# Two blocks of keys made behind the queries, closer steps in the attention, and two output blocks in turn

## The chip, the cores and the metric

One core of one Trainium2 chip runs the whole program. The metric is the device time in microseconds (us) of one execution, and lower is better. The engines are TensorE (PE, with PEld for its weight loads), VectorE (DVE), ScalarE (ACT), GpSimd (POOL) and SyncE (SP), which issues the loads of the weights.

## The reference

The reference is a two-layer decoder trunk on 256 positions and a width of 2048, in float32. Layer one is a retention layer with an MLP; layer two is a multi-head latent attention (MLA) with an MLP. The part that the change touches is the MLA of layer two, with 16 heads:

```python
kv = (c_kv @ w_kv_up).reshape(b, s, MLA_HEADS, MLA_NOPE_DIM + MLA_V_DIM)
k_nope = rms_norm(kv[..., :MLA_NOPE_DIM], k_nope_norm)
v = kv[..., MLA_NOPE_DIM:]
...
c_q = rms_norm(h @ w_dq, q_norm)
q = (c_q @ w_uq).reshape(b, s, H, MLA_NOPE_DIM + MLA_ROPE_DIM)
q_nope = rms_norm(q[..., :MLA_NOPE_DIM], q_nope_norm)
q_pe = apply_rope(rms_norm(q[..., MLA_NOPE_DIM:], q_pe_norm), cos[:, :, None], sin[:, :, None])
...
p = jax.nn.softmax(sc, axis=-1).astype(v.dtype)
return jnp.einsum('bhqk,bkhd->bqhd', p, v)
```

The scores sc are the products of q_nope with k_nope plus those of q_pe with the one rotary key k_pe, masked causally. The result of all heads goes through w_o and is added to the residual stream.

## The kernel before, in words

All products in this stage run as three matmuls: a float32 operand is split into a high half in fp32r and the rest, the low half (split, line 188: ACT makes the high half at L191, DVE the low half at L192). Weights come in pieces. stream (L214) loads one piece with a DMA on SP's queue and splits it in two halves of which each has a tile wh and a tile wl; there are five buffers of each and four of the raw piece. piece (L241) multiplies a half in 12 matmuls (L252 to L254), so a piece has 24. A block is a product with one set of columns over all pieces (gemm, L412).

Around the pieces, steps of other work are put in by hand. later(n, fn) (L99) queues a step that is due n pieces from now; tick (L107) is called at the end of each piece and runs what is due; need(items, n) (L112) runs queued steps early when a piece wants an operand that isn't there. This makes the order in which the program is written; the build then sets the order within each engine, so that matmuls of a step can stand between those of a piece.

The attention goes in blocks of two heads, b = 0 to 7. In the order of the program:

- The keys and values: eight blocks of one piece each, with 512 columns (chunks of mla_w_kv_up, tiles ku). keyed (L960) copies keys (kn) and values (v) out of PSUM on ACT, sums squares on DVE (L972, L973), takes the root on POOL (kn_r, L181), scales the keys (L978), and two pieces later transposes them (kntp) and splits them into kt (L194, L195).
- The queries: eight blocks of three pieces each, with 384 columns (mla_w_uq, tiles uq). query (L997) runs at a block's end: ACT copies the queries out (qs, L1002) and their squares (qu, L1004), DVE sums them (sq, L1005 and L1006), POOL takes the root (qn_r), and DVE scales and rotates (L1013, L864 to L867, L1022, L1023, tiles qs, qu, qpp).
- Three pieces later its turn (L1026) transposes both parts on PE (qntp, qptp), and ACT and DVE make qt (a raw tile and its two halves) and qpe.
- Three pieces after that, score (L1039) makes 20 matmuls into s (L1049 to L1054), DVE adds the mask into p (L1059) and takes the negated maximum mx (L1064), ACT takes the exponential with its sums (L1069), DVE the reciprocal, and ACT scales (L1075).
- Three pieces later its turn (L1077) transposes p (ptp, L1082) and ACT copies it (pt, L1084); two pieces after that, values (L1090) makes ao (L1093, L1094) and splits it into ot (L191, L192), which is appended to o_act.
- The output block: gemm_blocks (L424) multiplies o_act with mla_w_o, in four blocks of 512 columns with four pieces each (tiles wo). The first two blocks share a start: three pieces of block 0, three of block 1, then the last piece of each. Piece g needs 2g + 2 entries of o_act. x_tiles (L139) brings the residual stream back with DMAs that POOL issues (L146).

Transposes, ptp and ao share two PSUM banks under the tag "tp", taken in turn; products of weights share four ("acc"); s takes a pair of banks of its own, of which there is one.

Of the kernel before, what the change touches and what calls it, by code (L numbers as in the profile page):

```python
# [68 lines left out]
def yoco(ctx: ExitStack, tc: tile.TileContext, a):  # L69
# [7 lines left out]
    def small(w, name):  # L77
        return pool.tile([P, w], F32, tag="small", bufs=36, name=name)
# [20 lines left out]
    def later(n, fn):  # L99
        queue.append((clock[0] + n, next(count), fn))  # L100
# [311 lines left out]
    def gemm(w, chunk0, act, nk, nb, name, done, before=None):  # L412

        acc = accs(nb, name)
        n = nk // 4
        for g in range(n - 1):
            piece(w, chunk0 + g, acc, act, g, nk, nb, name, before)
        last_piece(w, chunk0, acc, act, nk, nb, name, done, before)
# [5 lines left out]
    def gemm_blocks(w, chunk_of, act, nk, name, done):  # L424

        n = nk // 4
        first = [accs(512, f"{name}{b}") for b in range(2)]
        for b in range(2):
            for g in range(n - 1):
                piece(w, chunk_of(b) + g, first[b], act, g, nk, 512, f"{name}{b}")  # L430
        for b in range(2):
            last_piece(w, chunk_of(b), first[b], act, nk, 512, f"{name}{b}", lambda acc, b=b: done(b, acc))
        for b in range(2, NB):
            gemm(w, chunk_of(b), act, nk, 512, f"{name}{b}", lambda acc, b=b: done(b, acc))
# [436 lines left out]
    rc, ckv = [], []  # L871
# [88 lines left out]
    def keyed(acc, b):  # L960
        if b % 2 == 0:
            vs.append(act_tile(f"v{b}", F32))
        vt = vs[-1][:, b % 2].rearrange("p t (h c) -> p t h c", h=2)
        v_s.append(vt)
        kr = []
        s2 = small(2 * NT, f"skn{b}").rearrange("p (t i h) -> p t i h", t=NT, i=1)
        for t in range(NT):
            src = acc[t].rearrange("p (h c) -> p h c", h=2)
            k = f2k([2, 2, NOPE], f"kn{b}{t}")
            nc.scalar.activation(k[:, 0], src[:, :, 0:NOPE], AF.Copy, scale=rc[t])  # L970
            nc.scalar.activation(vt[:, t], src[:, :, NOPE:], AF.Copy, scale=rc[t])
            nc.vector.tensor_tensor(k[:, 1], k[:, 0], k[:, 0], op=ALU.mult)  # L972
            nc.vector.reduce_sum(s2[:, t, 0], k[:, 1], axis=AX.X)  # L973
            kr.append(k)
        rn = rstds(s2, [NOPE], f"kn{b}")
        for t in range(NT):
            k = kr[t]
            nc.vector.tensor_tensor(  # L978
                k[:, 1], k[:, 0], rn[:, t, 0].unsqueeze(2).to_broadcast([P, 2, NOPE]), op=ALU.mult
            )  # L980

        def turn():
            tp = transposed(lambda t, j: kr[t][:, 1, j], f"kntp{b}")
            kt = act_tile(f"kt{b}")
            split(kt[:, 0], kt[:, 1], tp, gain(G_KN))
            k_t.append(kt)

        later(2, turn)

    for b in range(8):  # L990
        gemm(a["mla_w_kv_up"], b, ckv, 4, 512, f"ku{b}", lambda acc, b=b: keyed(acc, b))


    nc.vector.tensor_scalar(gqn, gain(G_QN), scale, None, op0=ALU.mult)
    o_act = []

    def query(acc, b):  # L997
        qr, qu = [], []
        sq = small(4 * NT, f"sq{b}").rearrange("p (t i h) -> p t i h", t=NT, i=2)
        for t in range(NT):  # L1000
            q = f2k([2, 192], f"qs{b}{t}")
            nc.scalar.activation(q.rearrange("p h c -> p (h c)"), acc[t], AF.Copy, scale=rq[t])  # L1002
            u = f2k([2, 192], f"qu{b}{t}")
            nc.scalar.activation(u.rearrange("p h c -> p (h c)"), acc[t], AF.Square, scale=rq[t])  # L1004
            nc.vector.reduce_sum(sq[:, t, 0], u[:, :, 0:NOPE], axis=AX.X)  # L1005
            nc.vector.reduce_sum(sq[:, t, 1], u[:, :, NOPE:], axis=AX.X)  # L1006
            qu.append((q, u))
        r = rstds(sq, [NOPE, ROPE], f"qn{b}")
        for t in range(NT):
            q, u = qu[t]  # L1010
            for i, cols in enumerate((slice(0, NOPE), slice(NOPE, NOPE + ROPE))):
                n = cols.stop - cols.start
                nc.vector.tensor_tensor(  # L1013
                    q[:, :, cols], q[:, :, cols], r[:, t, i].unsqueeze(2).to_broadcast([P, 2, n]), op=ALU.mult
                )
            flat = u.rearrange("p h c -> p (h c)")
            pe = flat[:, 0 : 2 * ROPE]
            tmp = flat[:, 2 * ROPE : 4 * ROPE].rearrange("p (h c) -> p h c", h=2)
            pe_rope(pe.rearrange("p (h c) -> p h c", h=2), tmp, q[:, :, NOPE:], t, 1, 2)
            parts = f2k([2, 2, ROPE], f"qpp{b}{t}", F32R)  # L1020
            pe = pe.rearrange("p (h c) -> p h c", h=2)
            nc.vector.tensor_copy(parts[:, :, 0], pe)  # L1022
            nc.vector.tensor_tensor(parts[:, :, 1], pe, parts[:, :, 0].bitcast(F32), op=ALU.subtract)  # L1023
            qr.append((q, parts.bitcast(F32)))

        def turn():  # L1026
            tp = transposed(lambda t, j: qr[t][0][:, j, 0:NOPE], f"qntp{b}")
            raw = f2k([2, S], f"qt{b}")
            nc.scalar.activation(raw, tp, AF.Copy, scale=gqn)
            qt = [f2k([2, S], f"qt{b}{i}", F32R) for i in range(2)]  # L1030
            split(qt[0], qt[1], raw)
            tp = transposed(lambda t, j: qr[t][1][:, j].rearrange("p i c -> p (i c)"), f"qptp{b}")
            qpe = f2k([2, S], f"qpe{b}", F32R)
            nc.scalar.copy(qpe, tp)
            later(3, lambda: score(b, qt, qpe))

        later(3, turn)

    def score(b, qt, qpe):  # L1039

        sc = two_banks(f"s{b}")
        for hh in range(2):
            for t in range(NT):
                dst = sc[:, hh, t * P : t * P + (t + 1) * P]
                qs = slice(t * P, (t + 1) * P)
                n = (t + 1) * P
                qh, ql = (i[:, hh, qs] for i in qt)
                kh, kl = (k_t[b][:, i, hh, :n] for i in range(2))
                nc.tensor.matmul(dst, qh, kh, start=True, stop=False)  # L1049
                nc.tensor.matmul(dst, qh, kl, start=False, stop=False)  # L1050
                nc.tensor.matmul(dst, ql, kh, start=False, stop=False)

                for i in range(2):
                    nc.tensor.matmul(dst, qpe[:, hh, qs], kpe_t[:, i, :n], start=False, stop=i == 1)  # L1054
        p = [f2k([2, (t + 1) * P], f"p{b}{t}") for t in range(NT)]
        for t in range(NT):
            cols = slice(t * P, t * P + (t + 1) * P)
            cut = mask[:, cols].unsqueeze(1).to_broadcast([P, 2, (t + 1) * P])
            nc.vector.tensor_tensor(p[t], sc[:, :, cols], cut, op=ALU.add)  # L1059
        neg = small(4, f"mx{b}")  # L1060
        den = small(4, f"den{b}")
        inv = small(4, f"inv{b}")
        for t in range(NT):
            nc.vector.tensor_reduce(neg[:, 2 * t : 2 * t + 2], p[t], axis=AX.X, op=ALU.max, negate=True)  # L1064
        for t in range(NT):
            for hh in range(2):
                i = 2 * t + hh
                view = p[t][:, hh]
                nc.scalar.activation(view, view, AF.Exp, bias=neg[:, i : i + 1], accum_out=den[:, i : i + 1])  # L1069
        nc.vector.reciprocal(inv, den)  # L1070
        for t in range(NT):
            for hh in range(2):
                i = 2 * t + hh
                view = p[t][:, hh]
                nc.scalar.activation(view, view, AF.Copy, scale=inv[:, i : i + 1])  # L1075

        def turn():  # L1077
            pt = []
            for hh in range(2):
                tp = bank("tp", [3 * P], f"ptp{b}{hh}")  # L1080
                for i, src in enumerate((p[0][:, hh], p[1][:, hh, 0:P], p[1][:, hh, P:])):
                    nc.tensor.transpose(tp[:, i * P : (i + 1) * P], src, ident)  # L1082
                o = f2k([3 * P], f"pt{b}{hh}")
                nc.scalar.copy(o, tp)  # L1084
                pt.append(o)
            later(2, lambda: values(b, pt))

        later(3, turn)

    def values(b, pt):  # L1090
        o = bank("tp", [2, S], f"ao{b}")
# [7 lines left out]
    for b in range(8):  # L1099
        gemm(a["mla_w_uq"], b * 3, cq, 12, Q_NB, f"uq{b}", lambda acc, b=b: query(acc, b))  # L1100

    ss = [small(NB, f"ss3_{t}") for t in range(NT)]
    act, r = [], []
    x_tiles("wo")
# [104 lines left out]
```

## Time and profile before

| what | us |
|---|---|
| median of 3 runs | 2476.02 (2473.25 to 2478.36) |
| the profiled execution | 2474.57 |
| its span in the trace | 2472.8 |
| keys and values, PE from - to | 1505 - 1552 |
| queries and attention, PE from - to | 1552 - 1684 |
| output block, PE from - to | 1684 - 1789 |

Times in the trace count from the start of the span. PE counts as busy from the start of a matmul to its modelled end, and matmuls overlap: the distance from one start to the next tells how fast they go. A line of the view of waits names the instruction that waited, what it waited for, the total, the number of times and the longest. In the windows each engine has its busy time and the number of instructions, then come PE's granted clock and the DMA share. The chain of waits names at each step the link that came last; its pieces are cut where the next one takes over, so its lengths add up.

### The profile page before, as it was taken

To read this page: it belongs to the slowest core of one execution; us is meant where nothing else is said; L and a number is where in the kernel's file an instruction comes from. 1 tells how busy PE (TensorE), PEld (TensorE's weight loads), DVE (VectorE), ACT (ScalarE), POOL (GpSimd) and SP (SyncE) were. 2 spreads that over 40 slices of the span, in tenths; PEclk is the share of its full clock that TensorE was granted. 3 is DMA by queue.
4 is the path that set the end of the run, shared out by engine and by line. 5 is a ranking of instruction groups with operands and counts; after the bars stand their busy time and mean duration, and the time that the engine had idled before them with its cause. 6 is when DMAs were issued, how large, how long until landed. Compare 5 with 4: busy or idle time off the path is not lost.

```text
span 2472.8 us, 31782 instructions
## 1 busy us (share of the span) xinstructions
PE 2456.4 (99%) x11635; PEld 2057.7 (83%) x11635; DVE 2187.8 (88%) x2842; ACT 1616.3 (65%) x2275; POOL 249.3 (10%) x310
## 2 busy tenths in 40 slices
PE   9999999999999999999999999999999999999999
PEld 7888888888888888888888888998888888888887
DVE  7799999889899999999999988776689999999996
ACT  6566656556676667667666767676566666676663
POOL 7300011000010010110110101110000201101100
PEclk9999999999999999999999999999999999999999
DMA  9545567555565685684775555445645856857854
GB/s 327 212 173 206 185 206 242 194 194 206 198 235 182 209 262 215 208 258 172 247 262 200 191 208 189 153 154 179 199 175 199 262 212 207 269 202 226 265 193 153
DMA packets 93980, 521.05 MB, mean 211 GB/s; under 512 B 11136, under 2 KB 12288, under 8 KB 40576
## 3 DMA queue, kind: packets, MB, share of 16 engines
q1 hardware_dynamic: 72288, 472.56, 53.4%
q0 software_dynamic: 21248, 46.15, 8.5%
q8 instruction: 91, 1.49, 0.2%
q14 instruction: 65, 0.53, 0.1%
q10 hardware_dynamic: 288, 0.31, 0.0%
HBM read 479.14 MB, written 39.85 MB: 210 GB/s over the span
## 4 chain that ended last, share of the span: by engine, by line
PE 90%; DVE 5%; ACT 3%; issue 1%; POOL 1%; DMA 1%; SPq 0%; ACTq 0%; DVEq 0%; POOLq 0%
PE u_c L364 7%; PE u_c L363 7%; PE u_c L362 7%; PE d_c L364 6%; PE d_c L362 6%; PE d_c L363 6%; PE rk_acc L280 2%; PE rq_acc L280 2%; PE rp_c L362 2%; PE rp_c L363 2%; PE rp_c L364 2%; PE u_p L364 2%; PE u_p L363 2%; PE u_p L362 2%; PE d_p L362 2%; PE d_p L364 2%
## 5 line engine op out<-in xcount | busy, mean ns | idle before, releaser
L191 ACT CAST u_wh<-u_raw 128x1024 fp32r<-128x1024 f32 x362 | 348.1, 991 | 207.8 <-DVE u_raw L327 100.7
L191 ACT CAST d_wh<-d_raw 128x1024 fp32r<-128x1024 f32 x358 | 344.3, 993 | 202.6 <-DVE d_raw L327 94.0
L192 DVE TENSOR_TENSOR u_wl<-u_raw,u_wh 128x1024 fp32r<-128x1024 f32 x362 | 401.6, 1142 | 47.4 <-ACT u_wh L191 41.8
L192 DVE TENSOR_TENSOR d_wl<-d_raw,d_wh 128x1024 fp32r<-128x1024 f32 x358 | 397.4, 1144 | 40.3 <-ACT d_wh L191 35.6
L362 PE MATMUL u_c<-u_wh,n 128*128 128x512 f32 x706 | 276.4, 392 | 0.0
L363 PE MATMUL u_c<-u_wl,n 128*128 128x512 f32 x706 | 275.5, 390 | 0.0
L364 PE MATMUL u_c<-u_wh,n 128*128 128x512 f32 x706 | 275.0, 390 | 0.0
L362 PE MATMUL d_c<-d_wh,hid 128*128 128x512 f32 x654 | 256.0, 391 | 0.0
L363 PE MATMUL d_c<-d_wl,hid 128*128 128x512 f32 x654 | 255.3, 390 | 0.0
L364 PE MATMUL d_c<-d_wh,hid 128*128 128x512 f32 x654 | 254.8, 390 | 0.0
L191 ACT CAST rp_wh<-rp_raw 128x1024 fp32r<-128x1024 f32 (+1 forms) x166 | 160.7, 982 | 140.0 <-DVE rp_raw L327 64.6
L192 DVE TENSOR_TENSOR rp_wl<-rp_raw,rp_wh 128x1024 fp32r<-128x1024 f32 (+1 forms) x166 | 184.6, 1135 | 26.0 <-ACT rp_wh L191 23.7
L364 PEld LDWEIGHTS u_c<-u_wh,n 128*128 128x128 f32 x706 | 132.6, 188 | 27.3
L362 PEld LDWEIGHTS u_c<-u_wh,n 128*128 128x128 f32 x706 | 132.5, 188 | 27.1
L363 PEld LDWEIGHTS u_c<-u_wl,n 128*128 128x128 f32 x706 | 132.6, 188 | 26.7
L364 PEld LDWEIGHTS d_c<-d_wh,hid 128*128 128x128 f32 x654 | 122.8, 188 | 25.4
L362 PEld LDWEIGHTS d_c<-d_wh,hid 128*128 128x128 f32 x654 | 122.8, 188 | 25.1
L363 PEld LDWEIGHTS d_c<-d_wl,hid 128*128 128x128 f32 x654 | 122.8, 188 | 24.7
L156 POOL DMA_DIRECT2D xh<-d_c x48 | 41.6, 867 | 856.4 <-ACT d_c L379 854.4
L191 ACT CAST ro_wh<-ro_raw 128x1024 fp32r<-128x1024 f32 x88 | 85.7, 997 | 59.5 <-DVE ro_raw L327 25.6
L362 PE MATMUL rp_c<-rp_wh,a 128*128 128x512 f32 x286 | 111.8, 391 | 0.0
L363 PE MATMUL rp_c<-rp_wl,a 128*128 128x512 f32 x286 | 111.4, 390 | 0.2 <-DVE rp_wl L192 0.2
(515 smaller groups left out, 6100.7 us busy)
## 6 DMA issues: line engine op xcount, KB each, us to landing
u_raw<-in_mlp_w SPq DMA_DIRECT2D x128, 1024.0 KB, 5.3
d_raw<-in_mlp_w SPq DMA_DIRECT2D x120, 1024.0 KB, 4.9
rp_raw<-in_ret_w_gv SPq DMA_DIRECT2D x56, 1024.0 KB, 4.8
ro_raw<-in_ret_w_out SPq DMA_DIRECT2D x32, 1024.0 KB, 4.9
uq_raw<-in_mla_w_uq SPq DMA_DIRECT2D x24, 768.0 KB, 4.1
rq_raw<-in_ret_w_qk SPq DMA_DIRECT2D x16, 1024.0 KB, 5.2
rk_raw<-in_ret_w_qk SPq DMA_DIRECT2D x16, 1024.0 KB, 4.9
wo_raw<-in_mla_w_o SPq DMA_DIRECT2D x16, 1024.0 KB, 4.8
```

The lines of the kernel that those rows point to most:

```text
L156: nc.gpsimd.dma_start(x_home[t][2 * p + j], part, accum_op=ALU.add)
L191: nc.scalar.copy(h, src)
L192: nc.vector.tensor_tensor(l, src, h.bitcast(F32), op=ALU.subtract)
L280: nc.tensor.matmul(acc[f], wh[:, cols], a.rearrange("p i s -> p (i s)"), start=k == 0, stop=k == nk - 1)
L362: nc.tensor.matmul(dst, ah, bh, start=n == 0, stop=False)
L363: nc.tensor.matmul(dst, ah, bl, start=False, stop=False)
L364: nc.tensor.matmul(dst, al, bh, start=False, stop=n == total[key] - 1)
```

## The change

Three edits. The keys and values of blocks 6 and 7 are made behind the last block of queries instead of ahead of the first. The distances of the attention's four steps, which were 3, 3, 3 and 2 pieces, are 3, 2, 3 and 2 for blocks 0 to 5, 3, 4, 2 and 1 for block 6 and 2, 2, 2 and 2 for block 7. The first two output blocks take their first three pieces in turn. Lines behind L990 have numbers some five higher in the changed kernel.

```diff
         first = [accs(512, f"{name}{b}") for b in range(2)]
-        for b in range(2):
-            for g in range(n - 1):
+        for g in range(n - 1):
+            for b in range(2):
                 piece(w, chunk_of(b) + g, first[b], act, g, nk, 512, f"{name}{b}")
...
-    for b in range(8):
-        gemm(a["mla_w_kv_up"], b, ckv, 4, 512, f"ku{b}", lambda acc, b=b: keyed(acc, b))
+    def keys(heads):
+        for b in heads:
+            gemm(a["mla_w_kv_up"], b, ckv, 4, 512, f"ku{b}", lambda acc, b=b: keyed(acc, b))
+
+    keys(range(6))
...
+    waits = [(3, 2, 3, 2)] * 6 + [(3, 4, 2, 1), (2, 2, 2, 2)]
...
-            later(3, lambda: score(b, qt, qpe))
+            later(waits[b][1], lambda: score(b, qt, qpe))
 
-        later(3, turn)
+        later(waits[b][0], turn)
...
-            later(2, lambda: values(b, pt))
+            later(waits[b][3], lambda: values(b, pt))
 
-        later(3, turn)
+        later(waits[b][2], turn)
...
     for b in range(8):
         gemm(a["mla_w_uq"], b * 3, cq, 12, Q_NB, f"uq{b}", lambda acc, b=b: query(acc, b))
 
+
+    keys((6, 7))
     ss = [small(NB, f"ss3_{t}") for t in range(NT)]
```

## The prediction

> **What bounds the kernel now.** Read first the page's busy line and its chain that ended last, then what TensorE (PE) waited for, then the windows of the attention stage.
>
> ```profile
> PE 2456.4 (99%) x11635; PEld 2057.7 (83%) x11635; DVE 2187.8 (88%) x2842; ACT 1616.3 (65%) x2275; POOL 249.3 (10%) x310
> PE 90%; DVE 5%; ACT 3%; issue 1%; POOL 1%; DMA 1%; SPq 0%; ACTq 0%; DVEq 0%; POOLq 0%
> ```
>
> ```profile
> PE qptp L211 <- DVE ot L192: 1.9, 1, 1.9
> ...
> PE qptp L211 <- ACT qt L1029: 1.1, 1, 1.1
> ...
> PE wo_acc L252 <- ACT ot L191: 0.3, 1, 0.3
> ```
>
> ```profile
> 1505.00:1552.40 47.40, 47.40 (x226) 39.27 (x225) 39.45 (x78) 33.46 (x61) 9.54 (x11) 1.00 0.43 150
> ...
> 1610.00:1630.00 20.00, 18.09 (x116) 17.41 (x116) 15.65 (x43) 15.32 (x34) 2.31 (x1) 1.00 0.40 146
> ...
> 1645.18:1662.88 17.70, 17.70 (x115) 17.48 (x114) 13.59 (x37) 12.66 (x29) 2.31 (x1) 1.00 0.42 147
> ...
> 1681.00:1735.00 54.00, 52.44 (x287) 44.86 (x286) 31.66 (x58) 33.60 (x71) 4.86 (x7) 1.00 0.51 176
> ```
>
> PE is the bound, at a granted clock of 1.00. The change keeps every matmul, so all it can win is PE's idle time from the keys to the second output block: 20.00 - 18.09 = 1.91 us, and 54.00 - 52.44 = 1.56 us. That is **3.5 us**; with the matmuls that run on at a slower pitch around these waits I take 4.0. A block of queries (two heads, b = 0 to 7) costs PE **17.70 us**, and in the window of one it never waits. The other engines are idle for 4 us of it, so their sum is no limit. Their order may be. These are the pieces of the chain of waits in which PE is not the link:
>
> ```profile
> 1662.56 0.58 ACT qs L1002
> 1663.14 0.47 ACT qu L1004
> 1663.61 0.47 ACT qs L1002
> 1664.08 0.48 ACT qu L1004
> ...
> 1664.59 0.42 DVE sq L1005
> ...
> 1665.55 2.25 POOL qn_r L181
> 1667.83 0.96 DVE qs L1013 x3
> ...
> 1671.46 0.87 DVE uq_wl L192
> 1672.33 0.60 DVE qt L192
> 1672.93 0.93 DVE p L1059 x2
> 1673.86 0.34 DVE mx L1064
> 1674.22 1.87 ACT p L1069 x8
> ...
> 1676.93 1.49 ACT p L1075 x4
> ```
>
> PE's own timeline of the same block:
>
> ```profile
> 1662.88 0.60 PE L211 MATMUL qntp<-cst,qs 128*128 128x128 f32 x4
> ...
> 1663.67 0.31 PE L1049 MATMUL s<-kt,qt 128*128 128x128 f32 x1
> ...
> 1663.93 0.27 PE L1051 MATMUL s<-kt,qt 128*128 128x128 f32 x1
> ...
> 1666.05 0.34 PE L252 MATMUL uq_acc<-uq_wh,cq 128*128 128x384 f32 x1
> ...
> 1675.09 0.59 PE L1093 MATMUL ao<-pt,v 128*128 128x256 f32 x2
> ...
> 1676.31 0.42 PE L252 MATMUL uq_acc<-uq_wh,cq 128*128 128x384 f32 x1
> ```
>
> The scores s leave PE at 1666.05, yet VectorE (DVE) adds their mask (p) at 1672.93, behind this block's roots, qs, a weight low (uq_wl) and the low half of qt. It takes its work as it stands, and p is late by 7 us. That costs nothing now: the scores that p reads were made long before, from the qt of an earlier round. So no link of this chain comes back to PE.
>
> **The change part by part.**
>
> *Steps 3, 2, 3, 2.* Scores now come two pieces behind their transposes instead of three, in the same round in which qt is made. In the changed program PE runs: transposes of block b, 57 rows of the next queries, values (ao), the first two products of s, then the third, which needs qt's low half. DVE has: the next block's qs to qpp (15 small instructions) with **four weight lows** among and behind them, qt low, ot low, and p of these scores. ScalarE (ACT) has exp, qs of the next-but-one block, the scaling (L1075), then qu, qs, qu. So a ring closes which PE is part of: qs to roots to DVE's stretch to qt low to **PE's scores** to p to exp to the next qs. One turn, from the chain's rows:
>
> - ACT: qs 0.58, scaling 1.49, qu, qs, qu 1.42: 3.49.
> - last qu's end to DVE's first qs (sums, POOL's root): 1667.83 - 1664.56 = 3.27.
> - DVE's small instructions: 1671.46 - 1667.83 = 3.63, less 0.3 for gaps that lows now fill; four lows at 0.87, 3.48; qt 0.60. In all 7.41.
> - PE: s from its third product, 1666.05 - 1663.93 = 2.12, and the second set of p's transposes inside it. These take the "tp" bank that ao had (two banks in turn), so they wait for ot's low half, which stands right behind qt's on DVE:
>
> ```profile
> L192 DVE TENSOR_TENSOR ot<-ao,ot x8: 681/683/690, 1627.1 to 1733.7; 128x512 fp32r<-128x512 f32 x8
> ```
>
>   0.68, less the products that run meanwhile: with 0.25 for the transposes 2.7 together.
> - p 0.93, mx to exp 0.36, exp 1.87: 3.16.
>
> Sum 3.49 + 3.27 + 7.41 + 2.7 + 3.16 = **20.0 us against 17.70**. Nothing hides this: PE is inside the ring, and what it could do meanwhile stands behind s in its queue. So 2.3 us are waited in each settled round, blocks 3 and 4: 4.6.
>
> The other rounds by the same rows. *Block 0*: no p yet, but queries 1 must pass first: PE reaches the third product after 0.79 (transposes, 1663.67 - 1662.88), 49 rows at 0.177 and 0.4 more: 9.9 (the row pitch is 17.70 less transposes 0.79, s 2.38, ao 1.22 and ptp 0.5, over 72 rows). qt is there after qs to qu 2.0, less 0.35 that qs starts before the block ends, 3.27, small ones 3.33, three lows 2.61 and 0.60: 11.5. Wait 1.6. *Block 1*: its round holds the load of exp's table.
>
> ```profile
> 1602.75 0.34 DVE mx L1064
> 1603.15 1.28 ACT L1069
> 1604.45 1.87 ACT p L1069 x8
> ```
>
> From s0's end DVE gives uq32's low after p and mx 1.29, the load 1.28, exp 1.87, ACT's 3.49, the 3.27, small ones 3.0 and itself, 0.87: 15.1. PE wants it after 22 rows, transposes and 49 rows, 13.4: 1.7. The Trainium skill, page "ScalarE: Activation LUTs", section "What ACT_TABLE_LOAD costs", puts a load at about 1.28 us and a drain at 1.38 more. The row ends where exp starts, so the drain isn't seen here; by the page the time would be 1.4 us higher. *Block 2*: uq42's low likewise late (1.0), qt low later than s (1.7), and uq51's low stands between qt's and ot's, so p's transposes wait 1.2 more: 3.9. But here no weight low stands beside POOL's root, and that matters:
>
> ```profile
> 1506.84 0.55 POOL L171 TENSOR_TENSOR cq_r<-cq_m,neg_half 128x1 f32<-128x1 f32 x1
> ...
> 1509.39 1.23 DVE L192 TENSOR_TENSOR ku_wl<-ku_raw,ku_wh 128x1024 fp32r<-128x1024 f32 x1 [0.27 <-ACT ku_wh L191]
> 1509.48 1.54 POOL L171 TENSOR_TENSOR cq_r<-cq_m,neg_half 128x1 f32<-128x1 f32 x1
> ```
>
> The same root takes 0.55 alone and 1.54 beside a low, 1.0 more; I take 1.0 off, 2.9. (The Trainium skill, "GPSIMD Engine Reference", section "Key points", says that POOL shares its SBUF interfaces with VectorE and is held up by instructions of two SBUF inputs. By that rule too the root without a neighbour is quicker; the rows agree.) *Block 5*: between qt's and ot's low stand two key lows of 1.22 (row below): 1.5 for qt and 2.0 for ot, 3.5. Sum of the rounds: 1.6 + 1.7 + 2.9 + 4.6 + 3.5 = **14.3**.
>
> *Two key blocks behind the queries.* Their rows only move: 192 key matmuls in the 47.40 window beside 34 transposes of 0.1 each make 0.23 a row, 48 rows 11 us, at the same pitch at either place. Two loads of 1 MB move behind 24 on SP's queue, which runs ahead of use. On POOL the two roots kn_r come behind the first two x loads, 0.56 us each and long ready: nothing. What they move on DVE counts:
>
> ```profile
> L192 DVE TENSOR_TENSOR ku_wl<-ku_raw,ku_wh 128x1024 fp32r<-128x1024 f32 x13 | 15.4, 1219 | 2.2 <-ACT ku_wh L191 2.2
> L973 DVE TENSOR_REDUCE skn<-kn 128x2 f32<-128x256 f32 x16 | 6.7, 420 | 0.5
> ...
> L181 POOL TENSOR_TENSOR kn_r<-kn_m,neg_half 128x4 f32<-128x4 f32 x8 | 8.1, 1009 | 36.2 <-DVE kn_m L180 36.2
> ...
> L146 POOL DMA_DIRECT2D x_wo<-xh x8 | 4.4, 556 | 0.0
> ```
>
> The second set of p5's transposes waits for ot4's low. From the end of s5 DVE gets there over p, mx, exp 3.16, scaling and qu 1.49 + 2.0, roots 3.27 - 1.0 (no low beside), small ones 3.3, four lows 4.9, qt 0.6, four steps on the keys 1.5, ot 0.7: 19.9. PE over 12 rows 2.1, transposes 0.8, 48 key rows 11.1, ao 1.2, ptp 0.25, 10 output rows 2.3: 17.8. Wait 2.1; then 0.1 for kt7's low. **2.2 us** in the tail, bounds 0 and 5.
>
> *First two output blocks in turn.* The third and fourth pieces now need four values and the fifth six; no forced steps. It and the keys between remove the 1.56 us wait and with the new banks the 1.91: -4.0 in all, already counted.
>
> **Sum**: 14.3 + 2.2 - 4.0 = +12.5 us on the profiled execution's 2474.57 (span 2472.8 and 1.8 around it), which stands 1.5 below the median 2476.02: **2487.1 us**. Against the median as against this execution it is slower by more than 0.2% (5 us, about what a measurement can tell from no change).
>
> **Rivals.**
>
> *The ring fits after all (not slower).* One mechanism: DVE's stretch from the root to qt's low half. If its lows don't stand in the way the ring is 20.0 - 3 x 0.87 = 17.4, under 17.70; it decides at 2.3 us less than I count. For it: that stretch took 1672.93 - 1667.83 = 5.1 us today. Against it: the lows stand there in the program. Then only the old waits go: 2474.57 - 4.0 = 2470.6, and up to 2479 if 1.3 us stay in each of six rounds.
>
> *Lateness adds up.* Weight lows behind qs reach PE late in every round, as in blocks 1 and 2 (1.0 to 1.7 each, four more rounds: 5), and the tail at its upper bound (5 instead of 2.2): 2487.1 + 5 + 2.8 = 2494.9. For it: DVE is then never ahead of PE. Against it: each wait of PE at s gives DVE that time back.
>
> *Scores don't come earlier.* The build may place s so late that qt is there, as in block 1 (58 rows). Then only the bank waits (ot low, 0.5 in each of five rounds, 2.0 in block 5, 2.2 in the tail) stay: 2474.57 - 4.0 + 6.7 = 2477.3.
>
> **How the numbers follow.** Forecast 0.62 (2480 to 2492); adding up 0.18 (2492 to 2499); the ring fits 0.12; scores not earlier 0.08. The range leaves out most of the ring that fits and reaches over the adding up: 2476 to 2497. Faster by over 0.2% would need more than the 4.0 us there are to win: 0.03. Within 0.2%: the rest of the two small cases, 0.17. Slower: 0.80.
>
> **What would show it.** PE waiting for DVE qt L192 before s in blocks 2 to 5, some 2 us each, and for DVE ot before ptp; windows of a block of 19.5 to 21 us instead of 17.70, with DVE p waiting for PE s; a root (qn_r) of about 1.3 us in blocks 3 and 7; no wait of qptp for ot. Wrong if the blocks last 17.7, if PE's waits name weight lows throughout, or if the loss lies in the output stage.

## The result and the profile after

| | us |
|---|---|
| before, median of 5 runs beside it | 2475.55 (2473.25 to 2478.36) |
| after, median of 5 runs | 2485.43 (2483.46 to 2488.70) |
| ratio | 1.0042, 95% interval 1.0031 to 1.0053 |
| after, the profiled execution | 2485.17, span 2483.4 |

The changed kernel is slower by 9.9 us in the medians and by 10.6 between the two profiled executions. The forecast was 2487.1, in a range of 2476 to 2497. The busy line and the chain that ended last look as they did before:

```profile
PE 2461.1 (99%) x11635; PEld 2061.7 (83%) x11635; DVE 2185.8 (88%) x2842; ACT 1617.2 (65%) x2275; POOL 249.1 (10%) x310
PE 89%; DVE 5%; ACT 3%; issue 2%; POOL 1%; DMA 0%; ACTq 0%; SPq 0%; POOLq 0%
```

PE has the same 11635 matmuls, yet is busy for 4.7 us more, and the span grew by 10.6: nearly half of the loss is not idle time at all. What PE waited for, in the attention stage:

```profile
PE s L1056 <- DVE qt L192: 7.4, 5, 1.7
...
PE ptp L1087 <- DVE ot L192: 1.6, 1, 1.6
...
PE uq_acc L253 <- DVE uq_wl L192: 0.3, 1, 0.3
```

The third product of s waits for qt's low half in five rounds, the tail once for ot's, and qptp no longer waits for ot. Windows, cut at the starts of the query transposes and around two of the waits (columns as before: length, busy time of PE, PEld, DVE, ACT and POOL, then PE's granted clock):

```profile
1614.20:1618.03 3.83, 3.79 (x21) 3.79 (x22) 1.46 (x2) 0.48 (x1) 0.00 (x0) 0.62 0.78 270
...
1622.12:1641.26 19.14, 18.02 (x115) 17.47 (x114) 13.57 (x35) 12.37 (x26) 2.31 (x1) 1.00 0.35 124
1641.26:1660.91 19.65, 18.09 (x115) 17.43 (x114) 12.99 (x36) 12.88 (x29) 2.31 (x1) 1.00 0.41 148
...
1675.50:1680.13 4.63, 4.52 (x24) 4.32 (x25) 2.81 (x3) 0.96 (x2) 0.00 (x0) 0.63 1.01 366
```

A round of 115 matmuls took 17.70 and takes 19.14 and 19.65. After two of the waits the clock is granted at 0.62 and 0.63, so PE is busy there and slow. One turn of the ring, and some rows beside it that are used further down, in the timeline:

```profile
1576.62 1.28 ACT L1074 ACT_TABLE_LOAD   x1
1581.26 0.40 ACT L1074 ACTIVATE p<-p,mx 128x128 f32<-128x128 f32 x1 [3.35 <-DVE mx L1069]
...
1605.25 1.64 POOL L181 TENSOR_TENSOR qn_r<-qn_m,neg_half 128x8 f32<-128x8 f32 x1 [15.51 <-DVE qn_m L180]
...
1655.27 0.68 DVE L192 TENSOR_TENSOR qt<-qt,qt 128x512 fp32r<-128x512 f32 x1
...
1656.00 0.33 PE L1056 MATMUL s<-kt,qt 128*128 128x128 f32 x1 [1.56 <-DVE qt L192]
...
1658.68 1.02 DVE L1064 TENSOR_TENSOR p<-s,cst 128x256 f32<-128x256 f32 x2 [2.13 <-PE s L1059]
...
1660.74 0.34 PE L254 MATMUL uq_acc<-uq_wh,cq 128*128 128x384 f32 x1
...
1661.40 0.49 ACT L1074 ACTIVATE p<-p,mx 128x256 f32<-128x256 f32 x1
...
1661.89 0.56 ACT L1007 ACTIVATE qs<-uq_acc,cq_r 128x384 f32<-128x384 f32 x1
...
1665.13 1.56 ACT L191 CAST uq_wh<-uq_raw 128x768 fp32r<-128x768 f32 x2
...
1666.16 2.31 POOL L181 TENSOR_TENSOR qn_r<-qn_m,neg_half 128x8 f32<-128x8 f32 x1 [17.52 <-DVE qn_m L180]
1668.51 0.96 DVE L1018 TENSOR_TENSOR qs<-qs,qn_r 128x256 f32<-128x256 f32 x3 [1.53 <-POOL qn_r L181]
...
1675.36 2.35 DVE L192 TENSOR_TENSOR ku_wl<-ku_raw,ku_wh 128x1024 fp32r<-128x1024 f32 x2
1675.50 0.33 PE L1056 MATMUL s<-kt,qt 128*128 128x128 f32 x1 [1.66 <-DVE qt L192]
...
1676.74 0.90 PE L1087 MATMUL ptp<-cst,p 128*128 128x128 f32 x3
```

From one third product to the next is 1675.50 - 1656.00 = **19.50 us**, made up of PE's scores to p 2.68, p to the next qs on ACT 3.21, ACT's qs to the last qu 3.24 (where the next weight half starts), sums and root 3.38, and VectorE's stretch 6.99. Each piece is within 0.5 of the prediction's (2.7, 3.16, 3.49, 3.27, 7.41). PE is in the ring, and waits in it: the brackets of its third product name qt, those of p name PE's s. The exp is a link as well: qs starts at 1661.89, just as the last exp ends, although PE had ended that block's last product at 1661.08.

Where the time came from, from PE's starts (excess of each distance over the same matmuls at their usual pitch):

| round | predicted | wait | slow pitch beside it | slow clock |
|---|---|---|---|---|
| block 0 | 1.6 | 1.41 | 0.2 | |
| block 1 | 1.7 | 0.32 | 0.4 | |
| block 2 | 2.9 | 1.61 | 0.5 | 1.6 |
| block 3 | 2.3 | 1.12 | 0.3 | |
| block 4 | 2.3 | 1.56 | 0.3 | |
| block 5 | 3.5 | 1.66 | 0.2 | 1.8 |
| tail | 2.2 | 1.62 | 0.2 | |
| sum | 16.5 | 9.3 | 2.1 | 3.4 |

That is 14.8 us; with the 4.0 us of the old waits and their pitch taken off, 10.8, beside the 11.2 us by which the stage from the first key matmul to the next stage's first grew (284.07 to 295.23). The rest of the kernel is 0.6 shorter.

### The profile page after: what moved, and what is told of

Same layout as the page of the kernel before. It is cut to its first block, busy times and chain, and to the rows that moved or that the text cites. A ratio compares the mean times of both kernels' runs of the same rounds, so it can differ in the third digit from the quotient of the medians.

```text
span 2483.4 us, 31780 instructions
## 1 busy us (share of the span) xinstructions
PE 2461.1 (99%) x11635; PEld 2061.7 (83%) x11635; DVE 2185.8 (88%) x2842; ACT 1617.2 (65%) x2275; POOL 249.1 (10%) x310
## 4 chain that ended last, share of the span: by engine, by line
PE 89%; DVE 5%; ACT 3%; issue 2%; POOL 1%; DMA 0%; ACTq 0%; SPq 0%; POOLq 0%
PE u_c L364 7%; PE u_c L362 7%; PE u_c L363 7%; PE d_c L362 6%; PE d_c L364 6%; PE d_c L363 6%; PE rk_acc L280 2%; PE rq_acc L280 2%; PE rp_c L362 2%; PE rp_c L363 2%; PE rp_c L364 2%; PE u_p L364 2%; PE u_p L363 2%; PE u_p L362 2%; PE d_p L362 2%; PE d_p L364 2%
```

## The experiments

*Theory A*: scores two pieces behind their transposes put PE into a ring of queues that are kept in order (scores, p, exp, qs, roots, VectorE's small instructions and weight lows, qt's low half, scores), and its turn is longer than PE's work on a block. *Rivals*: the moved keys or the turns of the output blocks cost the time; or no ring, but simply too much work ahead of qt in each round.

**Which of the three edits?** Four kernels. *steps_only* has the steps alone:

```diff
-    keys(range(6))
+    keys(range(8))
...
-    keys((6, 7))
```

(and before's order of the output blocks).

> The kernel before with the changed steps alone (3, 2, 3, 2 for blocks 0 to 5, and the changed steps of blocks 6 and 7); all keys ahead, output blocks one after the other. Ring theory (PE stands in a ring of 20 us a block because its scores wait for the low half of qt on VectorE): the waits of s for DVE qt stay, 7 to 8 us in five or six waits, and some of them lower the granted clock; 2483 to 2488 us. Rival, that the two moved key blocks overload VectorE and make its work late: the waits of s for qt go to nearly nothing, 2472 to 2477 us.

Measured: 2485.70, ratio 1.0043 (1.0029 to 1.0057). PE's waits:

```profile
PE s L1056 <- DVE qt L192: 8.3, 6, 1.6
...
PE ptp L1087 <- DVE ot L192: 1.3, 1, 1.3
```

The steps alone cost all that the change costs.

*turns_only* is before with the first two output blocks in turn:

```diff
-        for b in range(2):
-            for g in range(n - 1):
+        for g in range(n - 1):
+            for b in range(2):
```

> The kernel before with the first two output blocks in turn alone. Ring theory: only the short waits at the start of the output block can go, 1.0 to 1.6 us less than before, 2473 to 2476 us; the 1.9 us wait of qptp for ot stays. Rival, that this edit brings the loss because values are read later and the two blocks hold their banks longer: 2480 us or more.

Measured: 2476.53, ratio 1.0005 (0.9996 to 1.0014), half a us above the first forecast.

```profile
PE qptp L211 <- DVE ot L192: 1.9, 1, 1.9
PE wo_acc L252 <- ACT ot L191: 1.3, 1, 1.3
```

No gain: of the 1.56 us of old idle time in the output stage the wait for qt went, and a wait of 1.3 for ot came. The wait of 1.9 is that of before, but here the clock fell after it:

```profile
1627.17:1630.17 3.00, 3.00 (x20) 3.00 (x20) 2.86 (x8) 2.75 (x6) 0.63 (x1) 0.70 0.67 204
```

*keys_only* moves the two key blocks and keeps the old steps (block 6 with scores at 4):

```diff
+    waits = [(3, 3, 3, 2)] * 6 + [(3, 4, 3, 2), (3, 3, 3, 2)]
...
+    keys((6, 7))
```

> The kernel before with the two key blocks behind the queries alone; the scores of block 6 come 4 pieces behind their transposes instead of 3, since their keys are not there earlier. Ring theory: s stands behind a whole round, so no wait of s for qt; the 1.9 us wait of qptp for ot stays, the waits in the output block go in part: 2472 to 2476 us. Rival, that the moved key blocks overload VectorE: 2480 to 2485 us with waits for weight lows or for kt.

Measured: 2473.96, ratio 0.9994 (0.9985 to 1.0003): no difference that the interval shows. Waits of 1.2 for ot in three places, 0.9 for pt and 0.4 for kt are left.

*three_back* is the changed kernel with the scores of blocks 0 to 5 at three pieces again:

```diff
-    waits = [(3, 2, 3, 2)] * 6 + [(3, 4, 2, 1), (2, 2, 2, 2)]
+    waits = [(3, 3, 3, 2)] * 6 + [(3, 4, 2, 1), (2, 2, 2, 2)]
```

> The changed kernel with blocks 0 to 5 at 3, 3, 3, 2 again, all else as changed. Ring theory: a block of queries is back at 17.7 us, no wait of s for qt, granted clock at 1.00 throughout; 2472 to 2476 us. Rival, that the loss comes from the other two edits: 2482 us or more.

Measured: 2476.19, ratio 1.0003 (0.9994 to 1.0012).

```profile
PE ao L1098 <- ACT qt L1034: 2.0, 1, 2.0
...
PE ptp L1087 <- DVE ot L192: 0.8, 1, 0.8
PE qptp L211 <- DVE ot L192: 0.7, 2, 0.6
```

One number in six places is worth the whole loss, and no wait of s for VectorE is left. Keys and turns are out as the cause. A new wait of 2.0 came, of the values for qt, and the clock stayed full after it.

**Is it a ring?** *no_root* leaves out the root of the queries' norm: qs is scaled by a constant, so that the norm is missing from the queries.

```diff
-        r = rstds(sq, [NOPE, ROPE], f"qn{b}")
+        r = ones_r
```

> The changed kernel without POOL's root of the queries' norm and the steps between the sums and it: the sums of squares are still taken, but qs is scaled by a constant, so the norm of the queries is left out of the output. This takes about 2.3 (root) and 0.5 to 1 (mean and handing over) from the piece of the ring between the last qu and the first qs on VectorE. Theory A, the ring: one turn of 19.1 to 19.7 falls by about 3 to below 17.70, so the s waits in blocks 2 to 5 go to under 0.3 each, the block windows come back to 17.7 to 18.0, total 2474 to 2478. Theory B, only VectorE's lows ahead of qt count: they stand behind the root in order, but VectorE fills the root's time with lows already, so the waits fall by less than 1 each, total 2480 to 2484.

Measured: 2473.51, ratio 0.9992 (0.9983 to 1.0001), half a us under theory A's range. No wait of s is left; a settled round, a little above the 18.0 forecast:

```profile
1617.85:1636.12 18.27, 18.00 (x115) 17.42 (x114) 13.04 (x33) 12.84 (x29) 0.00 (x0) 1.00 0.37 130
```

*no_lows* has no low halves of the query weights on VectorE. TensorE multiplies by the high half again in their place, so that it has as many products.

```diff
-                split(wh[:, i * m : (i + 1) * m], wl[:, i * m : (i + 1) * m], raw[:, lo : lo + m])
-            use(half, wh, wl)
+                if name.startswith("uq"):
+                    nc.scalar.copy(wh[:, i * m : (i + 1) * m], raw[:, lo : lo + m])
...
+            use(half, wh, wh if name.startswith("uq") else wl)
```

> The changed kernel in which VectorE makes no low halves of the query weights (left out of the computation: TensorE multiplies by the high half once more in their place, so that it has as many products as before). Four of these lows, 0.87 to 0.95 each, were counted in the ring. Theory A (they are in the ring): one turn falls from 19.1 to 19.7 by about 3.5, below the 17.70 that PE has to do, and the waits of s for VectorE vanish in blocks 2 to 4; block 0's three lows go too, its wait of 1.4 vanishes. Total 2472 to 2477. The other theory, that the lows only fill gaps (the time of POOL's root, the handing over), so that the small instructions alone set the time: waits fall by 0 to 0.5 a round, total 2482 to 2486.

Measured: 2474.47, ratio 0.9995 (0.9986 to 1.0004).

```profile
1617.46:1635.12 17.66, 17.66 (x115) 17.48 (x114) 8.22 (x29) 12.75 (x30) 1.64 (x1) 1.00 0.41 135
```

PE never waits in this round. One wait of s is left in the kernel, 0.85 in block 5, where lows of the keys stand ahead of qt. Both root and lows are in the path, as theory A has it; the lows do not merely fill gaps. But a kernel without a ring that has too much work ahead of qt would gain from these two edits as well. They show the path, not yet that it closes.

*root_twice* lengthens the same path: the root is taken twice.

```diff
         r = rstds(sq, [NOPE, ROPE], f"qn{b}")
+        r = rstds(sq, [NOPE, ROPE], f"qr{b}")
```

> The changed kernel with the root of the queries' norm taken twice on POOL, one after the other: 2.3 us more between the last qu and VectorE's first qs in every round, nothing else. Theory A, a ring without slack: each settled round grows by the whole 2.3, from 19.1 to 19.7 to 21.4 to 22.0, and blocks 0 to 5 wait 2.0 to 2.3 more each: 12 to 14 us, total 2497 to 2506 with what the clock gives away beside it. Theory B, only the lows ahead of qt count: VectorE takes one or two of them in the longer root's time, and each round grows by 0.5 to 1.3: total 2488 to 2493.

Measured: 2494.86, ratio 1.0078 (1.0065 to 1.0092), between the two forecasts: 9.4 above the changed kernel. PE's waits, then rows of POOL and of the VectorE instruction behind it:

```profile
PE s L1057 <- DVE qt L192: 11.7, 6, 3.0
...
PE uq_acc L253 <- DVE uq_wl L192: 1.7, 1, 1.7
```

```profile
1632.86 1.64 POOL L181 TENSOR_TENSOR qn_r<-qn_m,neg_half 128x8 f32<-128x8 f32 x1 [15.39 <-DVE qr_m L180]
1634.46 1.64 POOL L181 TENSOR_TENSOR qr_r<-qr_m,neg_half 128x8 f32<-128x8 f32 x1
...
1655.85 0.95 DVE L192 TENSOR_TENSOR uq_wl<-uq_raw,uq_wh 128x768 fp32r<-128x768 f32 x1
1657.24 1.63 POOL L181 TENSOR_TENSOR qr_r<-qr_m,neg_half 128x8 f32<-128x8 f32 x1
1658.91 0.96 DVE L1019 TENSOR_TENSOR qs<-qs,qr_r 128x256 f32<-128x256 f32 x3 [2.12 <-POOL qr_r L181]
```

The second root cost 1.64, not 2.3. The six rounds grew from 116.2 to 122.5 us, 1.0 each, which is theory B's amount; the rest of the 9.4 came outside them. B's mechanism is not seen, though. In the second turn shown VectorE did take a second low beside the roots (the row at 1655.85), but four lows still stand between its first qs and qt's low, as in the changed kernel, and from that qs to s it takes 7.32 us in both (1658.91 to 1666.23 here, 1648.68 to 1656.00 there). What differs is ScalarE's order: a qs of the next block stands ahead of the exp in four rounds (at 1607.54, 1626.39, 1648.91 and 1667.43), in the changed kernel in one (at 1600.48). Theory A's number assumed a ring without slack, and fails: the work around a longer link falls into another order.

*exp_later* cuts the ring between exp and the next qs: exp, reciprocal and scaling one piece later.

```diff
+        if b < 6:
+            later(1, soft)
+        else:
+            soft()
```

(`soft` holds exp, reciprocal and scaling.)

> The changed kernel with exp, reciprocal and scaling of blocks 0 to 5 put one piece behind the scores (the distance from scores to the transposes of p stays the same in all), so that ScalarE has qs, qu, qs, qu of the next-but-one block ahead of the exp. Nothing on VectorE's small instructions, weight lows or qt is removed. Theory A, a ring that goes through p, exp and the next qs: the ring is cut between exp and qs, the waits of s for VectorE fall from 1.1 to 1.7 a round to under about 0.7, total 2474 to 2480. Theory B, no ring, the lows that stand ahead of qt in each round are simply more than PE gives time for: the waits stay at 1.1 to 1.7 in each of blocks 0 and 2 to 5, total 2484 to 2487.

Measured: 2485.80, ratio 1.0042 (1.0030 to 1.0054), theory B's number. But the place moved:

```profile
PE ao L1104 <- ACT qt L1034: 8.0, 5, 1.8
...
PE s L1056 <- DVE qt L192: 1.4, 1, 1.4
```

```profile
1648.60 0.17 DVE L1076 RECIPROCAL inv<-den 128x4 f32<-128x4 f32 x1
...
1648.81 1.50 ACT L1081 ACTIVATE p<-p,inv 128x128 f32<-128x128 f32 x4 [1.65 <-DVE inv L1076]
...
1650.93 0.68 ACT L1034 ACTIVATE qt<-qntp,gqn 128x512 f32<-128x512 f32 x1
...
1651.66 0.70 PE L1104 MATMUL ao<-pt,v 128*128 128x256 f32 x2 [1.56 <-ACT qt L1034]
```

The waits of s in blocks 2 to 5 are gone, as theory A has it. That is not only because PE already waited at the values just ahead of s: VectorE's first qs now comes 4.96 us after the start of the query transposes (1641.08 to 1646.04), where the changed kernel has 7.42 (1641.26 to 1648.68), and qt's low half ends 2.8 us sooner in the round. The time was lost in another ring: the reciprocal now stands behind VectorE's small instructions, the scaling waits for it, qt stands behind the scaling on ACT, and the values wait for qt. By itself this run tells the theories apart by the place, not by the sum. So *exp_later_inv* makes that reciprocal on POOL:

```diff
-            nc.vector.reciprocal(inv, den)
+            if b < 6:
+                nc.gpsimd.tensor_tensor(inv, den, neg_one[:, 0:4], op=ALU.pow)
+            else:
+                nc.vector.reciprocal(inv, den)
```

> exp_later with the reciprocal of blocks 0 to 5 made by POOL (a power of -1) instead of VectorE. In exp_later the waits of s for VectorE were gone in blocks 2 to 5, but PE waited 1.4 to 1.9 at the values for ScalarE's qt, because the scaling waited 1.65 for the reciprocal, which stood behind VectorE's small instructions. Theory A (the time is lost in rings through queues kept in order; exp_later cut one and closed another over the reciprocal): with the reciprocal on POOL, ready about 1.3 to 1.6 sooner, the second ring is cut too, PE's waits at s and at the values fall to under 0.4 a round, the settled round from 19.96 to 17.7 to 18.4, total 2474 to 2479. Theory B (each round's work ahead of qt is simply too much for the time that two pieces give, whatever the order): waits stay at 1 to 1.6 a round at some place, total 2483 to 2487.

Measured: 2479.92, ratio 1.0018 (1.0009 to 1.0027), between the two forecasts.

```profile
PE ao L1109 <- ACT qt L1036: 4.3, 5, 1.0
```

```profile
1640.02 2.25 POOL L181 TENSOR_TENSOR qn_r<-qn_m,neg_half 128x8 f32<-128x8 f32 x1 [15.88 <-DVE qn_m L180]
1642.23 1.00 POOL L1079 TENSOR_TENSOR inv<-den,neg_one 128x4 f32<-128x4 f32 x1
...
1643.27 1.50 ACT L1086 ACTIVATE p<-p,inv 128x128 f32<-128x128 f32 x4 [1.05 <-POOL inv L1079]
```

A round of 19.96 came down to 19.11. VectorE lost only the 0.17 of the reciprocal in each round, and yet the waits fell by half: the place in the queue counts more than the amount of work, against theory B. But theory A expected too much, and about 1.0 a round is left. The second ring was made shorter, not cut: on POOL the reciprocal stands behind the root and takes 1.00, so the scaling still waits 1.05 for it, and on ACT the exp, the scaling and three weight halves stand between qs and qt. No version on this path came under before.

**Can qt's low half be taken off VectorE?** *qt_low_pool* (from the changed kernel) and *keys_pool* (from keys_only) make it on POOL:

```diff
-            split(qt[0], qt[1], raw)
+            nc.scalar.copy(qt[0], raw)
+            nc.gpsimd.tensor_tensor(qt[1], raw, qt[0].bitcast(F32), op=ALU.subtract)
```

> The changed kernel with the low half of qt made by POOL instead of VectorE (ScalarE still makes the high half). Theory A, the ring through VectorE's queue: VectorE's stretch loses the 0.60 of qt and, more than that, the lows that stand ahead of qt no longer delay the scores; one turn of the ring falls under the 17.70 of a block, so the waits of s for VectorE (7.4 us over five rounds) vanish and the clock dips after them too. POOL is idle there, so its subtraction, even at twice VectorE's 0.60, costs 0 to 1 us a round at most: 2474 to 2478, against 2485.4. Theory B, it is only a waiting time for qt of whatever engine (qt itself is simply made too late, because its transposes come late): s then waits for POOL in place of VectorE, about as long or longer: 2484 to 2488.

Measured: 2490.86, ratio 1.0059 (1.0045 to 1.0074), above both forecasts; its six runs spread widely, from 2484.19 to 2496.46.

```profile
PE s L1057 <- POOL qt L1037: 10.3, 6, 4.4
```

```profile
1576.09 1.33 POOL L1037 TENSOR_TENSOR qt<-qt,qt 128x512 fp32r<-128x512 f32 x1 [4.55 <-ACT qt L1036]
...
1655.65 1.84 POOL L1037 TENSOR_TENSOR qt<-qt,qt 128x512 fp32r<-128x512 f32 x1 [3.92 <-issue]
1656.26 1.31 DVE L1027 CAST qpp<-qu 128x128 fp32r<-128x128 f32 x1
...
1674.10 5.62 POOL L1037 TENSOR_TENSOR qt<-qt,qt 128x512 fp32r<-128x512 f32 x1 [4.14 <-issue]
```

POOL's subtraction lasts 1.33 to 5.62 us in blocks 0 to 5, longest where four lows of the keys run on VectorE meanwhile, and VectorE is slower beside it too (the cast qpp 1.31, elsewhere 0.22 or 0.23). Where it took 1.83 and 1.84 the waits fell to 0.41 and 0.42 and the rounds to 18.23 and 18.24, so the ring did shorten, but in blocks 1, 2 and 5 it took 3.39, 2.88 and 5.62. Theory A's bound of twice VectorE's time was wrong.

> Before's steps 3, 3, 3, 2 and its single order of output blocks, with two key blocks behind the last queries, and qt's low half made by POOL. A version without the ring: VectorE has 0.60 less in each block. Theory A: nothing of the 7.4 us is there, and of the 3.5 us of old waits those for qt and ot shrink: 2472 to 2475, between 0.0 and 0.15 % under before. Theory B, that POOL's longer time for qt brings a wait of its own at s: 2477 to 2482.

Measured: 2474.91, ratio 0.9998 (0.9989 to 1.0006): within the first forecast, without a wait at s, and no gain over before: three waits of qptp for ot, 3.3 us in all, stayed.

## Why the prediction was right, and where it was not

*The ring (20.0 us a turn)*: right in sign, place and turn; the turns are 19.84 (1636.16 to 1656.00) and 19.50. The one before them, from block 2 to 3, is 21.92, with PE's scores at the slow clock in it. The two kernels that take a link's work out of it (no_root, no_lows) end its waits but for one of 0.85, the one that takes PE out of it (three_back) ends all, and exp_later, which moves one link and takes out none, ends those of blocks 2 to 5 and closes another ring. So the rival in which the ring fits falls; that lateness adds up falls too, since no round names a weight low but block 1's; and so does the rival in which scores don't come earlier, since PE stands at the third product in five rounds.

*The second set of p's transposes waits for ot's low half*: wrong in the rounds. The transposes at 1676.74 start while VectorE is still at ku_wl (1675.36 to 1677.71), ahead of ot's low. Only the tail has such a wait, 1.62. In the other rounds too these transposes start before that low half ends; why the bank is free by then stays open. The 2.7 for PE's link was right by chance: its 2.68 is the scores and the way to p.

*Blocks 3 and 4 (2.3 each)*: mis-sized. The prediction set PE's rows between two scores at one block, but the build moved the place: 79 rows of the next queries between the third products of blocks 2 and 3, seven over 72, or 1.2 us at 0.177. So the wait was 1.12 there; with 73 rows in the next turn it was 1.56.

*Block 0 (1.6)*: right, 1.41 and 0.2 beside it. *Block 1 (1.7)*: a wait of 0.32. The load of exp's table ran at 1576.62, ahead of mx; after it ACT stood idle for another 3.35 us until exp began at 1581.26. So the load's 1.28 should not have stood in that sum (15.1 less 1.28 is 13.8, PE's 13.4 beside it). In the kernel before the load came behind mx, although ACT stood idle for 2.9 us ahead of it. Why it ran early in one kernel and late in the other stays open.

*Block 2 (2.9)*: its one wait was 1.61 for qt (a term of 1.7); the 1.0 for uq42's low and the 1.2 for p's transposes did not come, and the clock gave 1.6 more. *Block 5 (3.5)*: 1.5 for qt was right (1.66), the 2.0 for ot did not come, and the clock gave 1.8. With the pitch both rounds lost 3.7: that the sums came near is luck, a slow clock in place of waits that did not come. *The root without a neighbour*: in blocks 3 and 7, as forecast, but 1.64 (the row at 1605.25) against 2.31: 0.7, where 1.0 was taken off.

*Tail (2.2)*: right, 1.62 and 0.2 beside it. *Old waits (-4.0)*: qptp's 1.9 went, and with the steps alone too (steps_only), so the moved keys were not needed for that; and the table above closes to 0.4 us with all 4.0 taken off. But the turns of the output blocks do not earn 1.56 by themselves (turns_only).

*The moved keys at the same pitch*: right, keys_only shows no cost.

So 12.5 was forecast and 10.6 came. Before the old waits are taken off, 16.5 was forecast, and 11.4 came of waits and pitch and 3.4 of the clock: the waits were taken too long by 5.1, and a term of 3.4 was missing. The sum is nearer than its parts, and in that it was lucky.

## What to carry to other kernels

Before a consumer is moved up to its producer, look for the ring that the move closes, through every queue that is kept in order, and compare its turn with the bound engine's work in a round: slack that looks free in the windows may be what keeps the ring open. An edit that cuts one ring (exp_later) can close the next, so follow the place of the wait and not only the sum. When a link is made longer or shorter, the work around it can fall into another order, so count on less than the whole.

## What the runs showed of the hardware

*The granted clock after a wait.* In the attention stages of the thirteen kernels the 3 us after a wait of PE had a full clock after all 15 waits of 0.8 to 1.2 us, a mean of 0.51 after one of three waits of 1.3 us, of 0.56 to 0.71 after 6 of 25 waits of 1.4 to 2.3 us, and 0.50 to 0.63 after all 4 of 2.6 to 4.4 us. Right behind the wait of 2.61 in qt_low_pool:

```profile
1598.63:1601.63 3.00, 3.00 (x15) 3.00 (x15) 0.00 (x0) 0.48 (x1) 0.00 (x0) 0.50 0.50 201
```

In the changed kernel such a drop cost 1.6 and 1.8 us, as much as the wait itself. The same wait of 1.9 had it in turns_only and not in before, so its length does not decide alone. The Trainium skill, page "TensorE: Matmul & The Clock Gate", Part 1, says that the gate knows a full and a half rate and looks at free-running windows of some 3.4 us: the 0.50 agrees, and windows that start anywhere would explain the chance in it. It asks for an idle window, though, and waits half as long were enough here; what decides stays open.

*POOL beside VectorE.* The Trainium skill, "GPSIMD Engine Reference", section "Key points", has POOL share its SBUF interfaces with VectorE. The runs agree and give sizes: 1.33 to 5.62 for one subtraction, 1.64 for the root with no weight low beside it and 2.2 to 2.3 with one.
